# Transposing the feed-forward activations on VectorE in 32-partition blocks in place of TensorE

## The chip, the core and the metric

The kernel runs on one core of one Trainium2 chip. Its engines are TensorE (PE: matmuls; PEld is its weight load), VectorE (DVE), ScalarE (ACT), GpSimd (POOL) and SyncE (SP, which issues most DMAs). The metric is the time of one execution on the device, in microseconds; lower is better.

## The reference

One layer of a diffusion transformer over 256 latent tokens and 256 context tokens, width 2048, all in float32. The change touches only the feed-forward part, whose inner width is 5632:

```
def swiglu_sublayer(x, shift, scale, gate, norm_g, w_ff_gate, w_ff_up, w_ff_down):
    h = modulate(rms_norm(x, norm_g), shift, scale)
    return x + gate * ((jax.nn.silu(h @ w_ff_gate) * (h @ w_ff_up)) @ w_ff_down)
```

Before it stand the modulation vectors, one input projection, two kinds of attention, and the projections that merge them. `x` here has 256 rows, so `h @ w_ff_gate` is 256x2048 by 2048x5632.

## The kernel before

Every large product is done by `project`, in float32 split into two parts that TensorE takes at its quick float32 rate: a high part (a rounded copy) and the remainder. A product is the sum of three matmuls: high x high, high x remainder, remainder x high (`mm3`, lines 211 to 214, the names L212, L213 and L214 of the profile). L213 reads the weights' remainder.

Weights come in **weight tiles** of 256 rows by 512 columns (`load_w`, line 198). For each, SyncE issues a DMA into `wraw` (seven buffers), ScalarE makes the high part `whi` (L207, three buffers) and VectorE the remainder `wlo` (L208, three buffers). With each weight tile TensorE does twelve matmuls of 128x512: six for the first 128 tokens (tk 0), six for the others (tk 1). With three buffers, ScalarE can cast a tile only when TensorE has finished the tile three places ahead of it; VectorE follows ScalarE.

The feed-forward loop goes over eleven **groups** (`cg`) of 512 inner columns. A group has eight gate tiles and then eight up tiles. At the end of the gate tiles ScalarE writes silu of each token half to `act` (L941); at the end of the up tiles VectorE multiplies that by the up product (`u_evac`, L944). `act[tk]` is then 128 tokens by 512 inner columns. The down projection (four column groups of 22 weight tiles each) needs it with the inner columns on the partitions, so it has to be transposed, and then be split into the two parts again (`split`: ScalarE L217, VectorE L218) into `fT`. `turn` does this: four TensorE transposes of 128x128 against an identity matrix (L951) into PSUM, and the split out of PSUM. `after(n, fn)` and `tick` put it off by two weight tiles for tk 0 and three for tk 1, so that it stands in the next group's gate tiles (or in the down projection's first tiles, behind the last group).

From the third group on (`cg > 1`), VectorE also accumulates the modulation vector `a5` from a stream of weights, two pieces behind the gate tiles and two behind the up tiles (L393 for the first of a half, L395 for the others; written `ada` in the profile).

A scheduler places instructions on each engine's queue; each queue is run in order. In the tables that follow, the weight tiles of a group are counted from 0: tiles 0 to 7 are its gate tiles, 8 to 15 its up tiles.

Of the kernel before, what the change touches and what calls it, by code (L numbers as in the profile page):

```python
# [17 lines left out]
P = 128  # L18
D = 2048
NKT = D // P  # L20
# [14 lines left out]
CG = 512  # L35
# [5 lines left out]
TURN = 3  # L41
TURN2 = 5
# [3 lines left out]
def hybrid_block(ctx: ExitStack, tc: tile.TileContext, t: dict, out: bass.AP):  # L46
    nc = tc.nc
# [9 lines left out]
    def big_tile(name, dt=F32):  # L57
        return big.tile([P, 2048], dt, tag="big", name=name)

    def mm_ps(name="mm"):  # L60
        return psum.tile([P, CG], F32, tag="mm", bufs=4, name=name)

    def tp_ps(name="tp"):
        return psum.tile([P, CG], F32, tag="tp", bufs=2, name=name)
# [4 lines left out]
    def scratch(name, n=CG, dt=F32, tag="scr", bufs=3):  # L69
        return scr.tile([P, n], dt, tag=tag, bufs=bufs, name=name)  # L70
# [5 lines left out]
    ident = tab.tile([P, P], F32, name="ident")  # L76
# [121 lines left out]
    def load_w(src, r0, c0, nk=WK, in_big=False):  # L198
        raw = wp.tile([P, WK, CG], F32, tag="wraw", bufs=WRAW, name="wraw")
        nc.sync.dma_start(out=raw[:, 0:nk], in_=src[r0:r0 + nk * P, c0:c0 + CG].rearrange("(k p) c -> p k c", p=P))  # L200
        if in_big:
            both = big_tile("wbig", F32R).rearrange("p (h k c) -> p h k c", h=2, c=CG)
            hi, lo = both[:, 0], both[:, 1]
        else:
            hi = wp.tile([P, WK, CG], F32R, tag="whi", bufs=WHI, name="whi")
            lo = wp.tile([P, WK, CG], F32R, tag="wlo", bufs=WLO, name="wlo")
        last_hi.append(nc.scalar.copy(out=hi[:, 0:nk], in_=raw[:, 0:nk]))  # L207
        last_lo.append(nc.vector.tensor_tensor(out=lo[:, 0:nk], in0=raw[:, 0:nk], in1=hi[:, 0:nk].bitcast(F32), op=ALU.subtract))  # L208
        return hi, lo

    def mm3(ps, ah, al, wh, wl, first, last):
        nc.tensor.matmul(ps, lhsT=ah, rhs=wh, start=first, stop=False)  # L212
        nc.tensor.matmul(ps, lhsT=ah, rhs=wl, start=False, stop=False)  # L213
        return nc.tensor.matmul(ps, lhsT=al, rhs=wh, start=False, stop=last)  # L214

    def split(hi, lo, src):
        nc.scalar.copy(out=hi, in_=src)  # L217
        nc.vector.tensor_tensor(out=lo, in0=src, in1=hi.bitcast(F32), op=ALU.subtract)  # L218
# [165 lines left out]
    def ada_pieces(a, chunk):  # L384

        for kt, hf in [(kt, hf) for kt in range(NKT) for hf in range(2)]:
            wt = wp.tile([P, 1024], F32, tag="wraw", bufs=WRAW, name="wada2")
            nc.sync.dma_start(out=wt, in_=w_ada[kt * P:(kt + 1) * P, chunk * D + hf * 1024: chunk * D + (hf + 1) * 1024])
            dst = a[:, hf * 1024:(hf + 1) * 1024]
            yield None  # L390
            with tc.issue_after(last_lo[-1].ins):
                if kt == 0:
                    nc.vector.tensor_scalar(out=dst, in0=wt, scalar1=sc[:, 0, 0:1], scalar2=None, op0=ALU.mult)  # L393
                else:
                    nc.vector.scalar_tensor_tensor(out=dst, in0=wt, scalar=sc[:, 0, kt:kt + 1], in1=dst, op0=ALU.mult, op1=ALU.add)  # L395
# [94 lines left out]
    def take(gen, n):  # L490
        for _ in range(n):
            if next(gen, gen) is gen:
                return

    def drain(gen):
        for _ in gen:
            pass
# [9 lines left out]
    def after(n, fn):  # L507
        late.append([n, fn])

    def tick():  # L510
        for e in list(late):
            e[0] -= 1
            if e[0] <= 0:
                late.remove(e)
                e[1]()
# [59 lines left out]
    def project(src, hl, nkt, c0, evac, kt0=0, side=None, head=1, tail=1, hook=None):  # L575


        ps = [mm_ps() for _ in range(2)]
        nt = nkt // WK
        order = [(i, tk) for i in range(nt) for tk in range(2)]  # L580
        order[:2 * head] = [(i, tk) for tk in range(2) for i in range(head)]
        order[-2 * tail:] = [(i, tk) for tk in range(2) for i in range(nt - tail, nt)]
        wt = {}
        for n, (i, tk) in enumerate(order):
            if i not in wt:
                wt[i] = load_w(src, i * WK * P, c0, in_big=WHI <= i < head or nt - tail <= i < nt - WHI)
            wh, wl = wt[i]
            for j in range(WK):
                k = i * WK + j
                ah, al = hl.at(kt0 + k, tk * P, P)  # L590
                mm3(ps[tk], ah, al, wh[:, j], wl[:, j], k == 0, k == nkt - 1)
            if i == nt - 1 and (tail > 1 or tk == 1):
                for x in ([tk] if tail > 1 else range(2)):
                    evac(x, ps[x])
            if hook:
                hook(i, tk)
            if n % 2:
                tick()
                if side:
                    side()  # L600
                yield None
# [24 lines left out]
    def q_evac(qT, br):  # L626
        def f(tk, ps):
            o = norm_rope(ps, br, "q", tk)

            def turn():  # L630
                tp = tp_ps("qtp")
                for h in range(4):
                    nc.tensor.transpose(out=tp[:, h * P:(h + 1) * P], in_=o[:, h * P:(h + 1) * P], identity=ident)
                src = tp.rearrange("p (h q) -> p h q", h=4)
                split(qT[:, 0, :, tk * P:(tk + 1) * P], qT[:, 1, :, tk * P:(tk + 1) * P], src)
            after(5 + tk, turn)
        return f
# [79 lines left out]
    def unit(br, u):  # L717
        return (u // 4, u % 4) if br == "a" else (u // 8, u // 2 % 4)
# [59 lines left out]
    for n, (br, u) in enumerate(units):  # L778
        q = (br, unit(br, u)[0])
# [33 lines left out]
    for cg in range(4):  # L813
# [19 lines left out]
        def gated(tk, ps):  # L833
            g = gs[tk]
            nc.vector.tensor_tensor(out=g, in0=ps, in1=g, op=ALU.mult)
            nc.vector.tensor_tensor(out=m[tk], in0=m[tk], in1=g, op=ALU.add)
            after(2 + tk, turn(tk))

        def turn(tk, cg=cg, m=m):
            def f():  # L840
                tp = tp_ps("mtp")
                for j in range(4):
                    nc.tensor.transpose(out=tp[:, j * P:(j + 1) * P], in_=m[tk][:, j * P:(j + 1) * P], identity=ident)
                hi, lo = mT.four(cg, tk * P, P)
                split(hi, lo, tp.rearrange("p (h q) -> p h q", h=4))
            return f
# [34 lines left out]
    hT = Parts("hT", NKT)  # L881
# [49 lines left out]
    w_g, w_u, w_d = t["w_ff_gate"][0], t["w_ff_up"][0], t["w_ff_down"][0]  # L931
    NFT = DFF // P
    fT = Parts("fT", NFT)
    for cg in range(DFF // CG):
        if cg == 2:
            a5 = big_tile("ada5")
            a5_gen = ada_pieces(a5, 5)
        act = [scratch(f"act{tk}") for tk in range(2)]

        def g_evac(tk, ps):  # L940
            nc.scalar.activation(out=act[tk], in_=ps, func=AF.Silu)  # L941

        def u_evac(tk, ps):
            nc.vector.tensor_tensor(out=act[tk], in0=ps, in1=act[tk], op=ALU.mult)  # L944
            after(2 + tk, turn(tk))

        def turn(tk, cg=cg, act=act):
            def f():
                tp = tp_ps("ftp")
                for j in range(4):  # L950
                    nc.tensor.transpose(out=tp[:, j * P:(j + 1) * P], in_=act[tk][:, j * P:(j + 1) * P], identity=ident)  # L951
                hi, lo = fT.four(cg, tk * P, P)
                split(hi, lo, tp.rearrange("p (h q) -> p h q", h=4))
            return f

        drain(project(w_g, hT, NKT, cg * CG, g_evac, **(dict(head=TURN2, hook=head_hook) if cg == 0 else {})))
        if cg > 1:
            take(a5_gen, 2)
        drain(project(w_u, hT, NKT, cg * CG, u_evac))
        if cg > 1:  # L960
            take(a5_gen, 2)
    drain(a5_gen)
# [2 lines left out]
    for cg in range(4):  # L965
        def d_evac(tk, ps):
            xr = scratch("xr2", tag="p", bufs=4)
            nc.gpsimd.dma_start(out=xr, in_=x2_d[tk, :, cg * CG:(cg + 1) * CG])
            y = scratch("y")
            nc.vector.tensor_tensor(out=y, in0=ps, in1=a5[:, cg * CG:(cg + 1) * CG], op=ALU.mult)  # L970
            nc.vector.tensor_tensor(out=y, in0=y, in1=xr, op=ALU.add)
            (nc.sync if cg == 3 else nc.gpsimd).dma_start(out=out[0, tk * P:(tk + 1) * P, cg * CG:(cg + 1) * CG], in_=y)
        drain(project(w_d, fT, NFT, cg * CG, d_evac, tail=TURN if cg == 3 else 1))


_INS = ["x", "c", "ctx", "c_ctx", "w_ada", "b_ada", "norm1_g", "w_in", "q_norm_a", "k_norm_a", "q_norm_b", "k_norm_b",
# [32 lines left out]
```

## Time and profile before

| | |
|---|---|
| median of 3 runs | 1733.82 us (1732.61 to 1733.86) |
| span of the profiled execution, first to last instruction | 1730.7 us |
| TensorE busy | 1706.1 us (99% of the span) |
| VectorE busy | 1132.6 us (65%) |
| ScalarE busy | 775.0 us (45%) |
| granted TensorE clock, mean over the span | 0.998 |
| the four transposes of one tile (L951), as one run of work | 0.60 us, 22 times |

The time of the profiled execution as a run is not listed by itself; its span is 3.1 us below the median, and that is taken as the same for both kernels. A busy TensorE is not one at its peak, since matmuls overlap: a 128x512 matmul lasts 0.39 us in the trace and the next one starts about 0.227 us after it.

### The profile page before, as it was taken

The numbers are of one execution on the slowest core, as the hardware profiler recorded it, in microseconds if no ns is written. First come the engines' busy times: TensorE is split into PE (matmuls) and PEld (weight loads), VectorE is DVE, ScalarE is ACT, GpSimd is POOL, SyncE is SP. The second block draws the span as 40 slices with busy tenths as digits, with TensorE's granted clock in tenths as the row PEclk, the third lists the DMA queues.
The fourth block names the chain that finished last, engine by engine and source line by source line (L and its number), as shares of the span: only waits on it lengthen the run. The fifth ranks groups of instructions, "written<-read, shape, count | busy, mean of one in ns | idle before, by whom it ended". The sixth has DMA issues, their size and how long they took to land.

```text
span 1730.7 us, 21827 instructions
## 1 busy us (share of the span) xinstructions
PE 1706.1 (99%) x8150; PEld 1378.5 (80%) x8150; DVE 1132.6 (65%) x1428; ACT 775.0 (45%) x1063; POOL 135.5 (8%) x204
## 2 busy tenths in 40 slices
PE   7999999999999999999999999999999999999998
PEld 5667778887787788888888788888888888888887
DVE  5754668888788879796665754555565665454554
ACT  5222223245656556667544444444444444333332
POOL 2100001001131120002110100000000000000000
PEclk9999999999999999999999999999999999999999
DMA  9877785687766676777796766677777777666662
GB/s 263 300 242 265 233 319 174 201 271 235 252 189 202 212 265 217 247 227 248 249 323 222 237 180 190 201 237 241 234 242 234 240 236 231 208 213 197 221 205 88
DMA packets 192010, 397.69 MB, mean 230 GB/s; under 512 B 13504, under 2 KB 25872, under 8 KB 191392
## 3 DMA queue, kind: packets, MB, share of 16 engines
q1 hardware_dynamic: 183952, 369.71, 66.2%
q0 software_dynamic: 7952, 26.58, 4.8%
q8 instruction: 64, 1.05, 0.2%
q14 instruction: 42, 0.34, 0.1%
HBM read 385.72 MB, written 10.52 MB: 229 GB/s over the span
## 4 chain that ended last, share of the span: by engine, by line
PE 88%; DVE 5%; issue 3%; DMA 1%; ACT 1%; POOL 1%; SPq 0%; DVEq 0%; ACTq 0%; POOLq 0%
PE mm L212 26%; PE mm L213 26%; PE mm L214 26%; PE ada L268 2%; DVE wlo L208 1%; PE ptp L687 1%; PE o L705 1%; DMA wraw<-in_w_in_dram 1%; PE ftp L951 1%; PE s L667 1%; ACT whi L207 1%; PE o L213 0%; PE o L214 0%; PE o L212 0%; PE s L212 0%
## 5 line engine op out<-in xcount | busy, mean ns | idle before, releaser
L208 DVE TENSOR_TENSOR wlo<-wraw,whi 128x1024 fp32r<-128x1024 f32 (+1 forms) x506 | 611.6, 1210 | 460.2 <-ACT whi L207 458.8
L207 ACT CAST whi<-wraw 128x1024 fp32r<-128x1024 f32 (+1 forms) x506 | 527.7, 1043 | 796.6 <-PE mm L214 682.0
L213 PE MATMUL mm<-wlo,hT 128*128 128x512 f32 x696 | 271.0, 389 | 2.0 <-DVE wlo L208 2.0
L212 PE MATMUL mm<-whi,hT 128*128 128x512 f32 x696 | 272.8, 392 | 0.0
L214 PE MATMUL mm<-whi,hT 128*128 128x512 f32 x696 | 271.3, 390 | 0.1
L212 PE MATMUL mm<-whi,xT 128*128 128x512 f32 x640 | 257.2, 404 | 0.6 <-ACT whi L207 0.6
L213 PE MATMUL mm<-wlo,xT 128*128 128x512 f32 x640 | 251.5, 393 | 0.9 <-DVE wlo L208 0.9
L214 PE MATMUL mm<-whi,xT 128*128 128x512 f32 x640 | 250.5, 392 | 0.0
L213 PEld LDWEIGHTS mm<-wlo,hT 128*128 128x128 f32 x696 | 130.7, 188 | 28.8 <-DVE wlo L208 2.4
L214 PEld LDWEIGHTS mm<-whi,hT 128*128 128x128 f32 x696 | 130.6, 188 | 27.9 <-DVE hT L218 0.5
L395 DVE SCALAR_TENSOR_TENSOR ada<-wada,sc,ada 128x1024 f32<-128x1024 f32 x120 | 152.0, 1277 | 0.0
L212 PEld LDWEIGHTS mm<-whi,hT 128*128 128x128 f32 x696 | 130.7, 188 | 26.3
L212 PEld LDWEIGHTS mm<-whi,xT 128*128 128x128 f32 x640 | 120.1, 188 | 37.3 <-issue 9.8
L213 PEld LDWEIGHTS mm<-wlo,xT 128*128 128x128 f32 x640 | 120.8, 189 | 25.1 <-DVE wlo L208 2.4
L214 PEld LDWEIGHTS mm<-whi,xT 128*128 128x128 f32 x640 | 120.3, 188 | 25.4
L212 PE MATMUL mm<-whi,fT 128*128 128x512 f32 x352 | 137.2, 390 | 0.0
L214 PE MATMUL mm<-whi,fT 128*128 128x512 f32 x352 | 137.0, 389 | 0.0
L213 PE MATMUL mm<-wlo,fT 128*128 128x512 f32 x352 | 136.9, 389 | 0.0
L212 PEld LDWEIGHTS mm<-whi,fT 128*128 128x128 f32 x352 | 66.1, 188 | 14.5 <-issue 0.8
L212 PE MATMUL mm<-whi,cT 128*128 128x512 f32 x192 | 75.5, 393 | 1.8 <-ACT cT L344 1.8
L214 PEld LDWEIGHTS mm<-whi,fT 128*128 128x128 f32 x352 | 66.1, 188 | 13.9
L213 PEld LDWEIGHTS mm<-wlo,fT 128*128 128x128 f32 x352 | 66.1, 188 | 13.4
(237 smaller groups left out, 2115.2 us busy)
## 6 DMA issues: line engine op xcount, KB each, us to landing
wada<-in_w_ada_dram SPq DMA_DIRECT2D x192, 512.0 KB, 4.6
wraw<-in_w_in_dram SPq DMA_DIRECT2D x154, 512.0 KB, 4.6
wraw<-in_w_ff_gate_dram SPq DMA_DIRECT2D x88, 512.0 KB, 4.5
wraw<-in_w_ff_up_dram SPq DMA_DIRECT2D x88, 512.0 KB, 3.8
wraw<-in_w_ff_down_dram SPq DMA_DIRECT2D x88, 512.0 KB, 4.8
wraw<-in_w_br_a_dram SPq DMA_DIRECT2D x32, 512.0 KB, 5.0
wraw<-in_w_out_dram SPq DMA_DIRECT2D x32, 512.0 KB, 5.1
wraw<-in_w_br_b_dram SPq DMA_DIRECT2D x16, 512.0 KB, 5.4
```

Source lines behind the costliest of these rows:

```text
L207: last_hi.append(nc.scalar.copy(out=hi[:, 0:nk], in_=raw[:, 0:nk]))
L208: last_lo.append(nc.vector.tensor_tensor(out=lo[:, 0:nk], in0=raw[:, 0:nk], in1=hi[:, 0:nk].bitcast(F32), op=ALU.subtract))
L212: nc.tensor.matmul(ps, lhsT=ah, rhs=wh, start=first, stop=False)
L213: nc.tensor.matmul(ps, lhsT=ah, rhs=wl, start=False, stop=False)
L214: return nc.tensor.matmul(ps, lhsT=al, rhs=wh, start=False, stop=last)
L268: last_pe[0] = nc.tensor.matmul(aps[32 * g:32 * g + 32, 0:ncol], lhsT=cst[:, k, :], rhs=rhs, start=(k < 4), stop=(k >= NKT - 4))
L395: nc.vector.scalar_tensor_tensor(out=dst, in0=wt, scalar=sc[:, 0, kt:kt + 1], in1=dst, op0=ALU.mult, op1=ALU.add)
L667: nc.tensor.matmul(sps[i], lhsT=qT[rows, x, hh, tk * P:(tk + 1) * P], rhs=kT["b", grp][y][rows, hh, :], start=(n == 0), stop=(n == 2))
L687: nc.tensor.transpose(out=tp[:, kt * P:(kt + 1) * P], in_=p[:, kt * P:(kt + 1) * P], identity=ident)
L705: nc.tensor.matmul(op[:, 0:BV], lhsT=pT[:, kt, :], rhs=vb[:, kt, hh * BV:(hh + 1) * BV], start=(kt == 0), stop=(kt == 3))
L951: nc.tensor.transpose(out=tp[:, j * P:(j + 1) * P], in_=act[tk][:, j * P:(j + 1) * P], identity=ident)
```

## The change

`turn` goes. In its place each `act[tk]` gets a generator, `turned`, that issues sixteen VectorE transposes of 32 partitions by 4 x 32 elements. Instruction (a, b) reads partitions 32a to 32a+31, takes column block b out of each of the four 128-column chunks, turns each 32x32 block, and writes to partitions 32b to 32b+31 of an SBUF tile `fturn`. Then the split reads `fturn` in place of PSUM. `project` calls `blocks_turned` behind each weight tile (its `side` argument), which takes four steps of the oldest generator.

```
+    chain = []
+
+    def blocks_turned():
+
+        for _ in range(4):
+            if chain and next(chain[0], chain) is chain:
+                chain.pop(0)
+
+    def turned(src, dst_hi, dst_lo):
+
+        whole = scratch("fturn", tag="sq", bufs=2)
+        sv = src.rearrange("p (k b j) -> p b k j", k=4, b=4)
+        dv = whole.rearrange("p (k a j) -> p a k j", k=4, a=4)
+        for a in range(4):
+            for b in range(4):
+                nc.vector.transpose(out=dv[32 * b:32 * b + 32, a], in_=sv[32 * a:32 * a + 32, b])
+                yield None
+        split(dst_hi, dst_lo, whole.rearrange("p (k q) -> p k q", k=4))
+
...
         def u_evac(tk, ps):
             nc.vector.tensor_tensor(out=act[tk], in0=ps, in1=act[tk], op=ALU.mult)
-            after(2 + tk, turn(tk))
-
-        def turn(tk, cg=cg, act=act):
-            def f():
-                tp = tp_ps("ftp")
-                for j in range(4):
-                    nc.tensor.transpose(out=tp[:, j * P:(j + 1) * P], in_=act[tk][:, j * P:(j + 1) * P], identity=ident)
-                hi, lo = fT.four(cg, tk * P, P)
-                split(hi, lo, tp.rearrange("p (h q) -> p h q", h=4))
-            return f
-
-        drain(project(w_g, hT, NKT, cg * CG, g_evac, **(dict(head=TURN2, hook=head_hook) if cg == 0 else {})))
+            chain.append(turned(act[tk], *fT.four(cg, tk * P, P)))
+
+        drain(project(w_g, hT, NKT, cg * CG, g_evac, side=blocks_turned, **(dict(head=TURN2, hook=head_hook) if cg == 0 else {})))
...
-        drain(project(w_u, hT, NKT, cg * CG, u_evac))
+        drain(project(w_u, hT, NKT, cg * CG, u_evac, side=blocks_turned))
...
-        drain(project(w_d, fT, NFT, cg * CG, d_evac, tail=TURN if cg == 3 else 1))
+        drain(project(w_d, fT, NFT, cg * CG, d_evac, side=blocks_turned, tail=TURN if cg == 3 else 1))
```

The new lines have the numbers L949 (transpose) and L963 (the multiplication that was L944). On TensorE the 22 runs of four L951 are gone and nothing else moves. What VectorE and ScalarE get to do, and in which order, is the scheduler's.

**VectorE, from the end of the third group's up tiles into the fourth group's gate tiles, before.** The first L208 rows are for tiles 2 and 3 of the fourth group.

```order
L944 TENSOR_TENSOR act_9592<-mm,act_9592 128x512
L944 TENSOR_TENSOR act_9593<-mm,act_9593 128x512
L208 TENSOR_TENSOR wlo<-wraw,whi 128x1024 x2
L218 TENSOR_TENSOR fT_9943<-ftp,fT_9943 128x4x128
L208 TENSOR_TENSOR wlo<-wraw,whi 128x1024
L218 TENSOR_TENSOR fT_9943<-ftp,fT_9943 128x4x128
L208 TENSOR_TENSOR wlo<-wraw,whi 128x1024 x3
L395 SCALAR_TENSOR_TENSOR ada_9591<-wada_9914,sc,ada_9591 128x1024
L395 SCALAR_TENSOR_TENSOR ada_9591<-wada_10082,sc,ada_9591 128x1024
L208 TENSOR_TENSOR wlo<-wraw,whi 128x1024 x8
```

Between two remainders there is at most one L218, or the two L395.

**The same place on VectorE with the change**, behind the two multiplications (`act_9622` is tk 0, `act_9623` is tk 1).

```order
L949 STREAM_TRANSPOSE fturn<-act_9622 32x4x32 x12
L208 TENSOR_TENSOR wlo<-wraw,whi 128x1024
L949 STREAM_TRANSPOSE fturn<-act_9622 32x4x32 x4
L208 TENSOR_TENSOR wlo<-wraw,whi 128x1024
L218 TENSOR_TENSOR fT_9957<-fturn,fT_9957 128x4x128
L949 STREAM_TRANSPOSE fturn<-act_9623 32x4x32 x3
L208 TENSOR_TENSOR wlo<-wraw,whi 128x1024
L949 STREAM_TRANSPOSE fturn<-act_9623 32x4x32 x4
L208 TENSOR_TENSOR wlo<-wraw,whi 128x1024
L949 STREAM_TRANSPOSE fturn<-act_9623 32x4x32 x8
L208 TENSOR_TENSOR wlo<-wraw,whi 128x1024
L949 STREAM_TRANSPOSE fturn<-act_9623 32x4x32
```

The five L208 rows are for tiles 2 to 6. The code asks for four transposes behind each weight tile; the scheduler puts twelve in one run ahead of tile 2's remainder, and eight ahead of tile 6's.

**What follows directly on VectorE with the change:**

```order
L218 TENSOR_TENSOR fT_9957<-fturn,fT_9957 128x4x128
L208 TENSOR_TENSOR wlo<-wraw,whi 128x1024
L395 SCALAR_TENSOR_TENSOR ada_9621<-wada_9968,sc,ada_9621 128x1024
L395 SCALAR_TENSOR_TENSOR ada_9621<-wada_10154,sc,ada_9621 128x1024
L208 TENSOR_TENSOR wlo<-wraw,whi 128x1024 x8
```

The second split has moved from ahead of tile 5's remainder to ahead of tile 7's, and the two L395, which stand where they stood, now come directly behind it. No wait stands between the transposes of one run.

**ScalarE, from one group's silu to the next one's, before:**

```order
L941 ACTIVATE act_9592<-mm 128x512
L941 ACTIVATE act_9593<-mm 128x512
L207 CAST whi<-wraw 128x1024 x10
L217 CAST fT_9943<-ftp 128x4x128
L207 CAST whi<-wraw 128x1024
L217 CAST fT_9943<-ftp 128x4x128
L207 CAST whi<-wraw 128x1024 x5
```

**and with the change:**

```order
L960 ACTIVATE act_9622<-mm 128x512
L960 ACTIVATE act_9623<-mm 128x512
L207 CAST whi<-wraw 128x1024 x10
L217 CAST fT_9957<-fturn 128x4x128
L207 CAST whi<-wraw 128x1024 x3
L217 CAST fT_9957<-fturn 128x4x128
L207 CAST whi<-wraw 128x1024 x3
```

The tenth L207 is tile 3 of the next group. The second L217 has moved from behind tile 4's cast to behind tile 6's; both L217 now wait for VectorE's sixteenth transpose, and the casts of tiles 4 and 7 stand behind them.

## The prediction

> **What bounds the kernel now.** I read first how busy each engine is, then the same for the middle of the feed-forward loop alone (stretches of the span; columns are length, busy time of each engine with its instructions, granted clock, DMA share), and then the order of time.
>
> ```profile
> PE 1706.1 (99%) x8150; PEld 1378.5 (80%) x8150; DVE 1132.6 (65%) x1428; ACT 775.0 (45%) x1063; POOL 135.5 (8%) x204
> ...
> core 0: us, PE busy (x) PEld busy (x) DVE busy (x) ACT busy (x) POOL busy (x), PEclk, DMA share, GB/s
> ...
> 1172.00:1477.00 305.00, 305.00 (x1374) 252.56 (x1374) 179.59 (x164) 130.33 (x138) 2.04 (x4) 1.00 0.75 236
> ```
>
> In those 305 us TensorE never stops, at full clock, while VectorE works 59% of the time. So an instruction taken from TensorE shortens the kernel by its whole place in the queue, as long as nobody makes TensorE wait in its stead. The order of time, around the first group's transposes (start, duration, engine, line, idle time ahead of it):
>
> ```profile
> 1037.69 1.23 DVE L208 TENSOR_TENSOR wlo<-wraw,whi 128x1024 fp32r<-128x1024 f32 x1 [1.50 <-ACT whi L207]
> ...
> 1038.83 1.28 DVE L944 TENSOR_TENSOR act<-mm,act 128x512 f32<-128x512 f32 x2
> ...
> 1039.12 0.39 PE L212 MATMUL mm<-whi,hT 128*128 128x512 f32 x1
> ...
> 1039.32 1.05 ACT L207 CAST whi<-wraw 128x1024 fp32r<-128x1024 f32 x1 [1.67 <-PE mm L214]
> ...
> 1040.41 1.23 DVE L208 TENSOR_TENSOR wlo<-wraw,whi 128x1024 fp32r<-128x1024 f32 x1 [0.29 <-ACT whi L207]
> ...
> 1041.39 0.39 PE L213 MATMUL mm<-wlo,hT 128*128 128x512 f32 x1
> ...
> 1041.62 0.39 PE L214 MATMUL mm<-whi,hT 128*128 128x512 f32 x1
> ...
> 1041.85 0.60 PE L951 MATMUL ftp<-ident,act 128*128 128x128 f32 x4
> 1042.04 1.05 ACT L207 CAST whi<-wraw 128x1024 fp32r<-128x1024 f32 x1 [1.67 <-PE mm L214]
> ...
> 1042.20 0.47 PE L212 MATMUL mm<-whi,hT 128*128 128x512 f32 x1
> ...
> 1042.51 0.39 PE L213 MATMUL mm<-wlo,hT 128*128 128x512 f32 x1
> ```
>
> Tile 0 of the second group starts at 1039.12 and has twelve matmuls, so without transposes tile 1 would start 12 x 0.227 = 2.72 us later. At 1039.32 ScalarE casts tile 2, when tile 7 of the up product is out of its buffer; VectorE follows at 1040.41 and ends at 1041.64, while tile 2 starts at 1039.12 + 5.44 = 1044.56. So VectorE can be some 3 us late with a remainder; that is the whole cover.
>
> **What goes: the transposes on TensorE.** From the L214 at 1041.62 to the second matmul behind the transposes, at 1042.51, are 0.89 us; two matmul places would be 0.45. A run of four costs 0.44 us of TensorE's queue, 0.88 a group, and the 22 runs 9.7 us. The split stays; it now reads SBUF:
>
> ```profile
> L217 ACT CAST fT<-ftp x22: 579/580/581, 1043.0 to 1492.0; 128x512 fp32r<-128x512 f32 x22
> L218 DVE TENSOR_TENSOR fT<-ftp,fT x22: 681/683/685, 1044.3 to 1493.3; 128x512 fp32r<-128x512 f32 x22
> ...
> L217 ACT CAST cT<-hx 128x512 fp32r<-128x512 f32 x7 | 4.3, 623 | 0.1
> ```
>
> ScalarE's half becomes 0.62 us (the row whose source is in SBUF, in place of 0.58), VectorE's stays at 0.69.
>
> **What comes: 352 transposes on VectorE.** The trace has none. Rows with 128 elements a partition, and rows on how instructions follow each other:
>
> ```profile
> L108 DVE TENSOR_TENSOR ce<-ce,cin 32x128 f32<-32x128 f32 x1 | 0.3, 280 | 0.0
> ...
> L710 DVE SCALAR_TENSOR_TENSOR on<-o,rstdo,gsub 128x128 f32<-128x128 f32 x16 | 5.6, 350 | 7.4 <-POOL rstdo L128 7.3
> ...
> L343 DVE TENSOR_SCALAR hx<-xtp,mod,mod 128x128 f32<-128x128 f32 x4 | 1.6, 408 | 1.9 <-PE xtp L339 1.9
> ...
> 15.78 0.16 DVE L142 TENSOR_REDUCE ss_row<-ss_part 128x1 f32<-128x4 f32 x1
> 15.97 0.15 DVE L127 TENSOR_SCALAR rstd_row<-ss_row 128x1 f32<-128x1 f32 x1
> ...
> 18.83 0.29 DVE L345 TENSOR_TENSOR xT<-hx,xT 128x128 fp32r<-128x128 f32 x1
> 19.04 1.27 DVE L148 TENSOR_SCALAR tok<-tok,rstd_row 128x512 f32<-128x512 f32 x3
> ```
>
> Let T be the time from one transpose to the next. The lower bound is 0.21 us: a 128-element instruction at 18.83 is followed 0.21 us later by one that doesn't need it, with 0.08 of overlap. If nothing overlaps, T is the 0.28 of the one row of 32x128 plus the 0.03 from an end (15.94) to the next start (15.97): 0.31. The upper bound is 0.41 (the 128x128 row out of PSUM), with 0.35 between. I take 0.31. The shape is that of the 280 ns row, and every overlap in the trace is between instructions that begin on partition 0 and go element by element; here each one writes to another 32 partitions than the last, and the first column of a block can only leave when its last row is in.
>
> The Trainium skill's "VectorE: DVE Perf Modes", section "Two Vector instructions with no wait between them", says that an instruction is held until all earlier ones have finished when it starts on other partitions than the last in the same memory; all sixteen write elsewhere than their predecessor. The trace's nearest pair (0.21, overlapped) begins on the same partitions and can't test it; by the rule the lower bound falls away, by the pair the whole 9.7 us is won. The same page's section "The three transpose paths" gives 311 ns for 128x128 in bf16, the only price of a transpose there is; with that as T the sum would be the one below.
>
> **The walk through VectorE's queue.** Time zero is the start of tile 0 of a group (1039.12); tile k starts at 2.72k plus what was lost. Two things set the loss: how late a remainder ends, and when TensorE goes on after one. For the second the trace has a row:
>
> ```profile
> 993.73 1.21 DVE L208 TENSOR_TENSOR wlo<-wraw,whi 128x1024 fp32r<-128x1024 f32 x1
> ...
> 994.99 0.50 PE L213 MATMUL mm<-wlo,hT 128*128 128x512 f32 x1 [2.00 <-DVE wlo L208]
> ...
> 995.33 0.39 PE L214 MATMUL mm<-whi,hT 128*128 128x512 f32 x1
> ```
>
> The remainder ends at 994.94; the next but one matmul starts 0.39 later. In an undisturbed tile that one starts 0.45 behind the tile's start. So TensorE loses what the remainder ends later than 0.06 behind the tile's start. For VectorE's instructions I take duration less 0.09 to the next start (1037.69 to 1038.83 for 1.23), and 0.04 from an end to an instruction that waited for it. In the order of the queue, with T = 0.31:
>
> - The multiplications end at 0.99 (1038.83 plus 1.28 is 1040.11). Twelve transposes, started at 0.91, end at 4.63. Tile 2's remainder ends at 5.86; tile 2 starts at 5.44: 0.36 lost.
> - Four transposes end at 7.0, tile 3's remainder at 8.25; tile 3 starts at 8.52: in time. ScalarE's split of tk 0 runs from 7.06 to 7.68, VectorE's ends at 8.86.
> - Three transposes, tile 4's remainder ends at 10.94 (start 11.24); four, tile 5's ends at 13.33 (start 13.96): in time.
> - Eight transposes end at 15.7, tile 6's remainder at 16.96; tile 6 starts at 16.68: 0.22 lost.
> - The last transpose ends at 17.2. ScalarE's second split waits for it (17.23 to 17.85), and behind it stands the cast of tile 7, to 18.82; the remainder ends at 20.09, tile 7 starts at 19.62: 0.41 lost. Here a wait on ScalarE, not VectorE's work alone, sets the end.
> - In groups with `a5`, two pieces come next and end at 22.5; tile 8's remainder ends at 23.64, tile 8 starts at 22.75: 0.83 lost. Their price:
>
> ```profile
> 1122.97 1.28 DVE L395 SCALAR_TENSOR_TENSOR ada<-wada,sc,ada 128x1024 f32<-128x1024 f32 x1
> 1124.17 1.22 DVE L208 TENSOR_TENSOR wlo<-wraw,whi 128x1024 fp32r<-128x1024 f32 x1
> ```
>
> From tile 9 on VectorE has caught up (24.79 against 26.30). A crossing with two pieces loses 1.82 us and saves 0.88; one without loses 0.99. Of the eleven crossings seven have two pieces; two have none (into group 1 and into the down projection), and two have one short or single piece, which the slack takes. Sum: 7 x (1.82 - 0.88) + 4 x (0.99 - 0.88) = +7.0 us on the span of 1730.7, so 1737.7, and with the 3.1 us between span and median **1740.8 us**.
>
> Costed at nothing: the loads of `wraw` (SyncE waits for VectorE's remainder before it refills one of seven buffers; a load lands in 4.8 us in the slowest of these stages, by the median, and seven tiles are 19 us, so a delay of 4 is covered), `act` and `fturn` (their next use is most of a group later), and the last group's transposes (done by tile 8 of 22; the down projection needs that group at tile 20). POOL's queue isn't touched.
>
> ```profile
> wraw<-in_w_ff_down_dram SPq DMA_DIRECT2D x88, 512.0 KB, 4.8
> ```
>
> **Rivals.** The same walk with other values of T gives them all; losses per crossing with and without pieces are, at 0.25: 0 and 0; 0.28: 0.88 and 0.05; 0.30: 1.50 and 0.67; 0.35: 3.10 and 2.27; 0.41: 5.02 and 4.19.
>
> - *Overlapped transposes.* With T up to 0.25 no remainder is late, and the whole 9.7 us are won: 1724.1. For it: the pair at 18.83, and VectorE's 41% of idle time. Against it: what I said on blocks and partitions. It decides below T = 0.29, where gain and loss are equal; at 0.28 the sum is 4 x (0.05 - 0.88) = -3.3, 1730.5.
> - *A dearer transpose.* At 0.35 the sum is 7 x 2.22 + 4 x 1.39 = +21, 1755; at 0.41 it is 7 x 4.14 + 4 x 3.31 = +42, 1776. For it: rows L710 and L343. Against: both have operands in PSUM, and the transpose has none.
> - *The clock.* Waits could cost TensorE its clock on top. After the wait of 2.0 us that ended at 994.99 the clock was halved for 2.5 us; after one of 1.29 us it wasn't (the last row has TensorE's busy time, the clock 1.00 and DMA alone).
>
> ```profile
> 996.30:998.80 2.50, 2.50 (x7) 1.87 (x6) 2.19 (x4) 0.00 (x0) 0.27 (x1) 0.50 0.80 269
> ...
> 741.96 0.50 PE L214 MATMUL mm<-whi,oT 128*128 128x512 f32 x1 [1.29 <-DVE oT L218]
> ...
> 742.00:744.00 2.00, 2.00 (x9) 1.00 0.00 0
> ```
>
> My longest wait is 0.83, so I don't count on it; 1.25 us at each of eleven crossings would make 1740.8 + 14 = 1755.
>
> **How the numbers follow.** T between 0.30 and 0.33 (+3 to +14): 0.38, the likeliest, with 1740.8. T up to 0.25: 0.27. Between 0.25 and 0.30: 0.17, half of it faster by more than 0.2% (3.5 us, about what a measurement of this kernel can tell from no change). Dearer: 0.12. Clock: 0.06. Faster: 0.27 + 0.08 = 0.35. Same: the other 0.09 and 0.04 from the low end of the first case: 0.13. Slower: 0.52. The range goes from 1723, just below the whole gain, to 1756, which takes in T = 0.35 and the clock; left out are the dearest transposes and what I overlooked, about 0.13. My forecast's own case is 1737 to 1748.
>
> **What would show it.** L951 gone and TensorE's matmul count down by 88; transposes of 0.28 to 0.31 with starts 0.31 apart; TensorE waiting for `wlo` in tiles 2, 6, 7 and 8 of each group, with some 1.8 us a crossing, and waits of ScalarE's L217 on the transposes. No waits at all and starts 0.2 apart would show the first rival; waits in every tile from 2 to 8 the second. The prediction is wrong if T is off by 0.02 us: each 0.01 moves the time by about 3.5 us.

## The result and the profile after

| | before | after |
|---|---|---|
| median of 5 runs each | 1733.82 us (1732.61 to 1734.24) | 1747.77 us (1745.33 to 1749.64) |
| span of the profiled execution | 1730.7 us | 1746.0 us |
| granted TensorE clock, mean | 0.998 | 0.998 |

The changed kernel is slower: 1.0081 times the time before, with a 95% interval of 1.0069 to 1.0093, or +13.95 us by the medians. The forecast was +7.0.

Of the 15.3 us between the two spans, 2.3 lie ahead of the change: tile 0 of the second group starts at 1039.12 before and at 1041.41 after. From there to the start of the last matmul are 685.90 us before (to 1725.02) and 698.94 after (to 1740.35). So 13.0 us is what the traces have to explain. This stretch, from tile 0 of the second group to the last matmul, is given for the kernels below too. What lies ahead of it is the same program but scatters: in nine of the ten traces tile 0 starts between 1038.63 and 1041.41, and in the second experiment, which clears two buffers first, at 1043.46. The prediction's 3.1 us between span and median hold some of that scatter as well; the changed kernel's span is 1.8 us below the time of its own run.

First how busy each engine is (busy us, share, instructions), then the same stretch as before in the stretches of the span:

```profile
PE 1707.2 (98%) x8062; PEld 1365.2 (78%) x8062; DVE 1236.0 (71%) x1780; ACT 774.5 (44%) x1063; POOL 134.8 (8%) x204
...
1172.00:1477.00 305.00, 296.82 (x1275) 236.72 (x1274) 242.91 (x386) 125.44 (x133) 2.03 (x4) 1.00 0.69 226
```

TensorE has 88 matmuls fewer, but in the 305 us in which it never stopped before, it now stands idle for 8.2, at full clock. The waits from the feed-forward loop on (instruction, what it waited for, us in total, times, longest) name the reason:

```profile
ACT fT L217 <- DVE fturn L949: 92.6, 22, 5.3
...
PEld mm L213 <- DVE wlo L208: 27.7, 38, 1.1
...
PE mm L213 <- DVE wlo L208: 11.7, 38, 0.7
```

TensorE waits 38 times for a remainder. One crossing, from the third into the fourth group, in order of time on VectorE, with ScalarE's second split and the cast behind it. Tile 0 starts at 1131.76.

```profile
1131.47 1.28 DVE L963 TENSOR_TENSOR act<-mm,act 128x512 f32<-128x512 f32 x2
1132.67 3.77 DVE L949 STREAM_TRANSPOSE fturn<-act 32x128 f32<-32x128 f32 x12
1136.47 1.23 DVE L208 TENSOR_TENSOR wlo<-wraw,whi 128x1024 fp32r<-128x1024 f32 x1
1137.72 1.26 DVE L949 STREAM_TRANSPOSE fturn<-act 32x128 f32<-32x128 f32 x4
1139.02 1.22 DVE L208 TENSOR_TENSOR wlo<-wraw,whi 128x1024 fp32r<-128x1024 f32 x1
1140.16 0.69 DVE L218 TENSOR_TENSOR fT<-fturn,fT 128x512 fp32r<-128x512 f32 x1
1140.76 0.92 DVE L949 STREAM_TRANSPOSE fturn<-act 32x128 f32<-32x128 f32 x3
1141.72 1.23 DVE L208 TENSOR_TENSOR wlo<-wraw,whi 128x1024 fp32r<-128x1024 f32 x1
1142.97 1.25 DVE L949 STREAM_TRANSPOSE fturn<-act 32x128 f32<-32x128 f32 x4
1144.26 1.23 DVE L208 TENSOR_TENSOR wlo<-wraw,whi 128x1024 fp32r<-128x1024 f32 x1
1145.52 2.52 DVE L949 STREAM_TRANSPOSE fturn<-act 32x128 f32<-32x128 f32 x8
1148.07 1.23 DVE L208 TENSOR_TENSOR wlo<-wraw,whi 128x1024 fp32r<-128x1024 f32 x1
1149.33 0.31 DVE L949 STREAM_TRANSPOSE fturn<-act 32x128 f32<-32x128 f32 x1
...
1149.67 0.62 ACT L217 CAST fT<-fturn 128x512 fp32r<-128x512 f32 x1 [5.32 <-DVE fturn L949]
1150.20 3.10 ACT L207 CAST whi<-wraw 128x1024 fp32r<-128x1024 f32 x3
...
1150.32 0.69 DVE L218 TENSOR_TENSOR fT<-fturn,fT 128x512 fp32r<-128x512 f32 x1 [0.69 <-ACT fT L217]
1151.28 1.22 DVE L208 TENSOR_TENSOR wlo<-wraw,whi 128x1024 fp32r<-128x1024 f32 x1 [0.26 <-ACT whi L207]
1152.42 2.47 DVE L395 SCALAR_TENSOR_TENSOR ada<-wada,sc,ada 128x1024 f32<-128x1024 f32 x2
```

Twelve transposes in 3.77 us: they follow one another 0.315 us apart, with no overlap. The L208 rows are for tiles 2 to 7. The same crossing on TensorE:

```profile
1137.20 0.39 PE L212 MATMUL mm<-whi,hT 128*128 128x512 f32 x1
1137.75 0.50 PE L213 MATMUL mm<-wlo,hT 128*128 128x512 f32 x1 [0.16 <-DVE wlo L208]
1138.08 0.39 PE L214 MATMUL mm<-whi,hT 128*128 128x512 f32 x1
...
1149.35 0.50 PE L213 MATMUL mm<-wlo,hT 128*128 128x512 f32 x1 [0.43 <-DVE wlo L208]
...
1152.55 0.50 PE L213 MATMUL mm<-wlo,hT 128*128 128x512 f32 x1 [0.17 <-DVE wlo L208]
...
1156.08 0.50 PE L213 MATMUL mm<-wlo,hT 128*128 128x512 f32 x1 [0.51 <-DVE wlo L208]
```

These are tiles 2, 6, 7 and 8. In tile 2 the third matmul starts 0.88 us behind the first, where two places are 0.45: 0.43 lost, of which the row shows 0.16 as idle. So each wait costs its idle time plus 0.27, since the matmuls ahead of the wait and behind it no longer overlap; in tiles 6, 7 and 8 the difference is the same within 0.02. For the 38 waits that is 11.7 + 38 x 0.27 = 22.0 us lost, against the 9.7 saved: +12.3 of the 13.0.

The 38 are tiles 2, 6 and 7 in the ten crossings between two groups, tile 8 in the seven with two pieces, and in the crossing into the down projection tile 6 alone:

```profile
1517.59 0.50 PE L213 MATMUL mm<-wlo,fT 128*128 128x512 f32 x1 [0.69 <-DVE wlo L208]
```

### The profile page after: what moved, and what is told of

The parts are those of the page before. It is cut to its first block, busy times and chain, and to the rows that moved or that the text cites. A ratio compares the mean times of both kernels' runs of the same rounds, so it can differ in the third digit from the quotient of the medians.

```text
span 1746.0 us, 22002 instructions
## 1 busy us (share of the span) xinstructions
PE 1707.2 (98%) x8062; PEld 1365.2 (78%) x8062; DVE 1236.0 (71%) x1780; ACT 774.5 (44%) x1063; POOL 134.8 (8%) x204
## 4 chain that ended last, share of the span: by engine, by line
PE 72%; DVE 16%; issue 5%; DMA 3%; ACT 2%; POOL 1%; SPq 0%; ACTq 0%; DVEq 0%; POOLq 0%
PE mm L213 22%; PE mm L214 21%; PE mm L212 21%; DVE wlo L208 6%; DVE fturn L949 5%; DMA wraw<-in_w_in_dram 3%; ACT whi L207 2%; PE ada L268 1%; PE ptp L687 1%; PE o L705 1%; DVE act L963 1%; PE s L667 1%; PE o L213 0%; PE o L214 0%; PE o L212 0%
## 5 line engine op out<-in xcount | busy, mean ns | idle before, releaser
L208 DVE TENSOR_TENSOR wlo<-wraw,whi 128x1024 fp32r<-128x1024 f32 (+1 forms) x506 | 609.8, 1210 | 360.1 <-ACT whi L207 356.8
L207 ACT CAST whi<-wraw 128x1024 fp32r<-128x1024 f32 (+1 forms) x506 | 526.3, 1043 | 715.0 <-PE mm L214 592.2
L213 PE MATMUL mm<-wlo,hT 128*128 128x512 f32 x696 | 275.6, 396 | 13.0 <-DVE wlo L208 13.0
L395 DVE SCALAR_TENSOR_TENSOR ada<-wada,sc,ada 128x1024 f32<-128x1024 f32 x120 | 152.0, 1277 | 0.0
L949 DVE STREAM_TRANSPOSE fturn<-act 32x128 f32<-32x128 f32 x352 | 106.4, 302 | 5.3
L212 PEld LDWEIGHTS mm<-whi,fT 128*128 128x128 f32 x352 | 66.1, 188 | 14.7 <-issue 0.8
```

The lines of the kernel that those rows point to most:

```text
L949: nc.vector.transpose(out=dv[32 * b:32 * b + 32, a], in_=sv[32 * a:32 * a + 32, b])
```

## The experiments

The theory was that of the prediction: TensorE's saving is real, and the bunched, unoverlapped transposes make remainders late for more than that. The rivals: VectorE's added work itself is too much; the saving is less than it seems; the a5 pieces or ScalarE's queue have no part in it; writing to other partitions is not what keeps the transposes apart. In the diffs `-` and `+` are against the changed kernel. The median of the kernel before was 1734.2 us beside the first four kernels below and 1734.6 beside the others.

**No transposes on any engine.**

```
-            chain.append(turned(act[tk], *fT.four(cg, tk * P, P)))
+            hi, lo = fT.four(cg, tk * P, P)
+            after(2 + tk, lambda tk=tk, act=act, hi=hi, lo=lo: split(hi, lo, act[tk].rearrange("p (h q) -> p h q", h=4)))
```

> No engine transposes the activations: the split reads act as it stands, on the old schedule (this leaves the transposition out). Both theories: the 22 runs of four TensorE transposes were worth 22 x 0.44 = 9.7 us, so about 1724.1, and TensorE waits for no weight remainder in the feed-forward loop. If the gain was mis-sized (if TensorE had given part of it back elsewhere in any case), it is above 1728.

Measured: 1723.41 us (1722.82 to 1727.02), 0.9943 times before (0.9929 to 0.9956). TensorE doesn't wait for a remainder anywhere in the loop. The gain of taking the transposes off TensorE is real and of the size that the prediction had: 9.9 us by the ratio (7.6 to 12.3), 9.7 forecast. The stretch takes 675.56 us, 10.3 less than before, so a run of four was worth 0.47 us and not 0.44.

**All sixteen transposes on the same partitions.**

```
-        whole = scratch("fturn", tag="sq", bufs=2)
+        whole = wholes[0]
+        wholes.reverse()
...
-                nc.vector.transpose(out=dv[32 * b:32 * b + 32, a], in_=sv[32 * a:32 * a + 32, b])
+                nc.vector.transpose(out=dv[0:32, a], in_=sv[0:32, b])
```

(`wholes` are two `fturn` buffers, cleared once on GpSimd and used in turn.)

> All sixteen transposes read and write partitions 0 to 31 (this leaves three quarters of each turned tile out, they stay zero); number, size and type of the instructions are the change's. Theory: transposes start one behind the other without overlap because each goes to other partitions than the last. Then they now overlap, start some 0.22 us apart for the same 0.30 us, no remainder is late, and the time is about 1724. Rival: a transpose never overlaps with the next one, whatever its partitions. Then they stay 0.315 apart and the time stays at about 1748.

Measured: 1723.35 us (1720.7 to 1726.42), 0.9933 (0.9919 to 0.9947): as fast as without any transposes, and the stretch takes the same 675.56 us. The instructions of `fturn` as a group (count, shortest/median/longest ns), and the order of time on VectorE:

```profile
L953 DVE STREAM_TRANSPOSE fturn<-act x352: 256/257/300, 1044.4 to 1492.0; 32x128 f32<-32x128 f32 x176
...
1131.41 1.83 DVE L953 STREAM_TRANSPOSE fturn<-act 32x128 f32<-32x128 f32 x9
1133.17 1.17 DVE L208 TENSOR_TENSOR wlo<-wraw,whi 128x1024 fp32r<-128x1024 f32 x1
1134.28 1.25 DVE L953 STREAM_TRANSPOSE fturn<-act 32x128 f32<-32x128 f32 x6
1135.47 1.17 DVE L208 TENSOR_TENSOR wlo<-wraw,whi 128x1024 fp32r<-128x1024 f32 x1
```

Nine transposes of 0.257 take 1.83 us, so starts are (1.83 - 0.257) / 8 = 0.197 apart on the mean instead of 0.315. The remainder starts 0.07 before the last transpose ends (1131.41 + 1.83 against 1133.17), and the next transpose 0.06 before the remainder ends; in the changed kernel both start 0.02 to 0.03 after. The scheduler also put nine instead of twelve transposes ahead of tile 2's remainder here. That alone couldn't free tile 6: ahead of its remainder stand 31 transposes in both kernels. Since everything here begins on partition 0, the run doesn't tell whether transposes that stay on other partitions overlap too.

**Pieces of a5 three weight tiles later**, behind the third up tile instead of directly behind the gate tiles.

```
-        if cg > 1:
-            take(a5_gen, 2)
-        drain(project(w_u, hT, NKT, cg * CG, u_evac, side=blocks_turned))
+        for i, _ in enumerate(project(w_u, hT, NKT, cg * CG, u_evac, side=blocks_turned)):
+            if cg > 1 and i == 2:
+                take(a5_gen, 2)
```

> The two a5 pieces behind the gate tiles move to behind the third up tile; all else is the change's. Theory (late remainders, place by place): only tile 8's wait goes, 0.8 us at each of the seven crossings with two pieces, 5.6 us in all, to about 1742; waits in tiles 2, 6 and 7 stay as they are. Rival (VectorE has too much to do between two groups, wherever it stands): the pieces are still to be done there, and the time stays within 2 us of 1748.

Measured: 1740.84 us (1738.47 to 1742.06), 1.0034 (1.0021 to 1.0046). The waits:

```profile
PEld mm L213 <- DVE wlo L208: 21.2, 31, 1.1
...
PE mm L213 <- DVE wlo L208: 8.2, 31, 0.7
```

31 waits instead of 38: just the seven of tile 8 are gone, and with them 6.9 us by the medians and 5.7 in the stretch, which takes 693.25 us (seven waits of 0.78, as shown above, are 5.5). So tile 8's wait is the pieces'; the other three stand without them.

**Transposes spread and put off.** The chain starts three weight tiles later (`after(4, ...)` counts the tile in which it is called; the expectation says two), so that a group's first four transposes stand behind tile 2's remainder. Every transpose is held behind the latest remainder, which keeps runs at four.

```
-                nc.vector.transpose(out=dv[32 * b:32 * b + 32, a], in_=sv[32 * a:32 * a + 32, b])
+                with tc.issue_after(last_lo[-1].ins):
+                    nc.vector.transpose(out=dv[32 * b:32 * b + 32, a], in_=sv[32 * a:32 * a + 32, b])
...
-            chain.append(turned(act[tk], *fT.four(cg, tk * P, P)))
+            gen = turned(act[tk], *fT.four(cg, tk * P, P))
+            after(4, lambda gen=gen: chain.append(gen))
```

> The same sixteen transposes a tile, but started two weight tiles later and pinned, four each behind the remainder of the weight tile last issued, so that no run is longer than four or five. Theory (bunching): 1.26 us of transposes and 1.23 us of a remainder fit into a weight tile's 2.72 us, no remainder is late, and the whole 9.7 us is won: about 1724. Rival (VectorE's added 110 us, or its use of the memory, slow TensorE however they are spread): 1740 or more.

Measured: 1722.85 us (1720.66 to 1726.35), 0.9934 (0.992 to 0.9948). This version beats both kernels, and it is as fast as the one without transposes; the stretch takes 675.56 us once more. How busy the engines are, and VectorE at the same crossing:

```profile
PE 1695.5 (99%) x8062; PEld 1369.7 (80%) x8062; DVE 1238.2 (72%) x1780; ACT 776.2 (45%) x1063; POOL 135.3 (8%) x204
...
1128.22 1.22 DVE L208 TENSOR_TENSOR wlo<-wraw,whi 128x1024 fp32r<-128x1024 f32 x1 [0.30 <-ACT whi L207]
1129.36 1.24 DVE L950 STREAM_TRANSPOSE fturn<-act 32x128 f32<-32x128 f32 x4
1130.94 1.23 DVE L208 TENSOR_TENSOR wlo<-wraw,whi 128x1024 fp32r<-128x1024 f32 x1 [0.34 <-ACT whi L207]
1132.20 1.25 DVE L950 STREAM_TRANSPOSE fturn<-act 32x128 f32<-32x128 f32 x4
```

VectorE works as long as in the changed kernel (1238.2 us against 1236.0) with the same 352 transposes 0.315 apart. But remainder and four transposes now take 2.4 us of each tile's 2.72, VectorE waits 0.3 for the next cast, and TensorE waits for no remainder. So it isn't the amount of work on VectorE that made the change slow, but where it stands.

**Only the hold behind the latest remainder**, without the later start (the first of the two edits above).

> The change with the transposes only pinned behind the remainder of the weight tile last issued; the start isn't put off, so the run of twelve ahead of tile 2 stays (tiles 0 and 1 have their remainders by then) and the rest is spread by fours. Theory (walk through VectorE's queue with 0.315 us from start to start and no overlap where a remainder and a transpose follow each other): tile 2 loses 0.4 us at every crossing, tiles 6 and 7 nothing, tile 8 some 1.2 us at the crossings with two a5 pieces: 3.7 us above the kernel before, about 1737.5. Rival (pinning alone cures it, the later start isn't needed): 1724.

Measured: 1734.47 us (1733.15 to 1736.3), 1.0004 (0.9995 to 1.0012). Weight loads that waited at the crossing from the third group:

```profile
1133.64 0.19 PEld L213 LDWEIGHTS mm<-wlo,hT 128*128 128x128 f32 x1 [0.58 <-DVE wlo L208]
...
1151.10 0.19 PEld L213 LDWEIGHTS mm<-wlo,hT 128*128 128x128 f32 x1 [1.27 <-DVE wlo L208]
```

The run of eight ahead of tile 6 is gone, and tiles 6 and 7 no longer wait. Twelve still stand ahead of tile 2's remainder, and the pieces and a split ahead of tile 8's. The hold takes most of the loss back: the stretch takes 688.12 us, 2.2 more than before. The later start on top of it brings the rest of the gain; what it would do without the hold, no run shows.

**The split later.** Both halves of a split come three weight tiles later than in the change, held behind the latest cast and the latest remainder.

```
-        split(dst_hi, dst_lo, whole.rearrange("p (k q) -> p k q", k=4))
+        def parts():
+            src = whole.rearrange("p (k q) -> p k q", k=4)
+            with tc.issue_after(last_hi[-1].ins):
+                nc.scalar.copy(out=dst_hi, in_=src)
+            with tc.issue_after(last_lo[-1].ins):
+                nc.vector.tensor_tensor(out=dst_lo, in0=src, in1=dst_hi.bitcast(F32), op=ALU.subtract)
+        after(3, parts)
```

> The transposes stand as in the change, in the same runs, but both halves of the split come three weight tiles later, pinned behind the newest cast and remainder, so that ScalarE's cast of a weight tile never stands behind a wait for transposes. Theory: the waits at tiles 7 and 8 (0.5 and 0.8 us) hang on ScalarE's queue and go, tile 6 keeps a half (0.44), tile 2 its 0.4: 1.2 us above the kernel before, about 1735. Rival (VectorE's transposes alone make the remainders late, ScalarE only follows): 1744 or more.

Measured: 1733.62 us (1730.29 to 1739.67), 0.9992 (0.9981 to 1.0002).

```profile
1133.60 0.19 PEld L213 LDWEIGHTS mm<-wlo,hT 128*128 128x128 f32 x1 [0.57 <-DVE wlo L208]
...
1144.92 0.19 PEld L213 LDWEIGHTS mm<-wlo,hT 128*128 128x128 f32 x1 [0.53 <-DVE wlo L208]
```

The stretch takes 685.06 us, 0.8 less than before. The expectation took the transposes to stay in the change's runs. They don't: between the remainders of tiles 4 and 6 they now stand in runs of seven and six,

```profile
1138.23 2.20 DVE L949 STREAM_TRANSPOSE fturn<-act 32x128 f32<-32x128 f32 x7
1140.45 1.23 DVE L208 TENSOR_TENSOR wlo<-wraw,whi 128x1024 fp32r<-128x1024 f32 x1
1141.71 1.90 DVE L949 STREAM_TRANSPOSE fturn<-act 32x128 f32<-32x128 f32 x6
1143.64 1.23 DVE L208 TENSOR_TENSOR wlo<-wraw,whi 128x1024 fp32r<-128x1024 f32 x1
```

so the last one ends ahead of tile 6's remainder and not behind it.

Tile 2 waits as before, tile 6 less, and tiles 7 and 8 not at all, although the pieces stand where they stood. With no cast queued behind a split that waits for transposes, VectorE gets through in time. The edit moves ScalarE's half, VectorE's half and, by the scheduler, the last transposes together, so their shares aren't told apart.

**Half on VectorE.** tk 0 by VectorE as in the change, tk 1 by TensorE as before (`turn` as in the kernel before).

```
-            chain.append(turned(act[tk], *fT.four(cg, tk * P, P)))
+            if tk == 0:
+                chain.append(turned(act[tk], *fT.four(cg, tk * P, P)))
+            else:
+                after(2 + tk, turn(tk))
```

> Only the first token half of each group (tk 0) is turned on VectorE, the second on TensorE as before. Theory: 11 x 0.44 = 4.8 us are saved; the run of twelve ahead of tile 2 is there and would lose 0.4 us, but TensorE's own transposes of the second half stand just ahead of tile 2 and give it 0.44 more time, so nothing is lost: about 1729. Rival (each turned tile costs its share of the 24 us that were lost in all): 1734 + 7 = 1741.

Measured: 1727.43 us (1726.92 to 1728.89), 0.9957 (0.9945 to 0.9969). The twelve transposes still stand ahead of tile 2's remainder; TensorE's work there:

```profile
1132.70 1.23 DVE L208 TENSOR_TENSOR wlo<-wraw,whi 128x1024 fp32r<-128x1024 f32 x1
...
1133.44 0.60 PE L973 MATMUL ftp<-ident,act 128*128 128x128 f32 x4
1133.79 0.48 PE L212 MATMUL mm<-whi,hT 128*128 128x512 f32 x1
1134.11 0.39 PE L213 MATMUL mm<-wlo,hT 128*128 128x512 f32 x1
```

TensorE's own transposes of tk 1 fall just ahead of tile 2 and give its remainder, which ends at 1133.93, the time that it lacked. No matmul waits. Half the saving, 4.9 us, was expected on that; the stretch, 680.67 us, is 5.2 shorter than before, and the medians say 5.4 to 9.5 by the interval.

**Written partition kept over four transposes, read partition changed each time.**

```
-        for a in range(4):
-            for b in range(4):
+        for b in range(4):
+            for a in range(4):
```

> The two loops over a and b are swapped: four transposes in turn write to the same 32 partitions and read from changing ones; the result is the same. Theory A (a change of the partitions read or of those written holds the next transpose): starts stay 0.315 us apart, time about 1748. Theory B (only a change of the partitions written holds it): three of four overlap, starts some 0.22 us apart on the mean, no remainder is late, about 1724.

Measured: 1745.95 us (1743.83 to 1747.15), 1.0062 (1.0048 to 1.0076).

```profile
L949 DVE STREAM_TRANSPOSE fturn<-act x352: 289/303/309, 1041.1 to 1514.7; 32x128 f32<-32x128 f32 x176
...
1131.50 3.77 DVE L949 STREAM_TRANSPOSE fturn<-act 32x128 f32<-32x128 f32 x12
```

Nothing changes (the stretch takes 698.87 us against 698.94): a change of the partitions that are read holds a transpose as a change of those written does.

## Why the prediction was right in direction and short by half

- **What bounds the kernel, and the gain.** Right: without transposes 9.9 us are won (9.7 forecast; 10.3 in the stretch), and the version with the transposes spread and put off wins the same.
- **The price of a transpose, T.** 0.31 was taken between 0.21 and 0.41; the trace has 0.303 long and 0.315 apart. By the prediction's own 3.5 us for each 0.01, that is worth 1.7 us. The first rival (overlapped transposes) is refuted for this kernel, and the pair of rows that spoke for it does hold where the partitions stay: 0.197 apart in the second experiment. The Trainium skill's "VectorE: DVE Perf Modes", section "Two Vector instructions with no wait between them", says that an instruction waits until all earlier ones have finished if the partitions where its input or its output begins are in another quarter than the last time; the second and the eighth experiment agree with it (0.197 with none changed, 0.315 with the input's changed each time). By that rule a transpose behind a remainder, and a remainder behind a transpose, are held as well. A tile's first transpose isn't, since it reads and writes from partition 0 as the instruction ahead of it does; so fifteen of the sixteen are held.
- **The dearer transpose and the clock.** Neither came: T is 0.315, tiles 3 to 5 wait in no crossing, and the clock is the same 0.998.
- **The walk through the queue.** The tiles are the forecast ones, 2, 6, 7 and 8. Their losses:

| tile | 2 | 6 | 7 | 8 | crossing with pieces | without |
|---|---|---|---|---|---|---|
| forecast, us | 0.36 | 0.22 | 0.41 | 0.83 | 1.82 | 0.99 |
| measured, us | 0.43 | 0.70 | 0.44 | 0.78 | 2.35 | 1.57 |

("Without" is tiles 2, 6 and 7 of this crossing.) The crossing into the down projection is unlike the others: its one wait costs 0.69 + 0.27 = 0.96. With the measured losses the prediction's own sum is 7 x (2.35 - 0.88) + 3 x (1.57 - 0.88) + (0.96 - 0.88) = +12.4 of the 13.0 between the traces.

The step that failed is the size of tile 6's loss, which alone makes 10 x 0.48 = 4.8 us of the 6.0 by which the sum was short. More than half of what made it too small is one term of the walk: "For VectorE's instructions I take duration less 0.09 to the next start". It was read from two elementwise instructions in a row and used at every change between remainder and transposes. In the trace after, the remainder that starts at 1136.47 ends at 1137.70 and the transposes follow at 1137.72: 0.11 later than the prediction had it. Where both begin on partition 0 the 0.09 stands: the L218 at 1140.16 ends at 1140.85, and the first transpose of the next tile starts at 1140.76. Up to tile 6's remainder there are three runs of transposes directly behind a remainder (3 x 0.11 = 0.33), 31 transposes of 0.315 instead of 0.31 (0.16), and five remainders that start some 0.03 later than the steps of T allow (0.13): 0.62 together. Tile 6's remainder ends 17.54 behind tile 0's start (1149.30 less 1131.76), where 16.96 was forecast: 0.58 in fact. Tile 2 is only 0.08 of that late and loses 0.07 more, which gives the later tiles that much; the rest falls on tile 6, where no slack is left, and makes 0.22 into 0.70. The prediction argued from the partitions for T, within a run, and not at its ends. The second experiment, where starts at these changes come 0.06 to 0.07 before the end again, shows that it is the partitions.

- **ScalarE's queue and the pieces.** Borne out: in the trace after, tile 7's remainder waits for a cast that stands behind the second split (1149.67 to 1151.28), with the split later the waits of tiles 7 and 8 go, and with the pieces later that of tile 8 alone. The share of ScalarE's queue by itself wasn't isolated.
- **Costed at nothing.** Loads, buffers and the down projection's need of the last group cost nothing that shows: TensorE has no such wait from the loop on.

What stays open is small. By the medians four kernels came out 1 to 3 us below their expectation; the stretch, without the scatter ahead of it, leaves two. Later pieces gain 5.7 there (5.6 expected) and half the work 5.2 (4.8). The hold alone comes out 2.2 above the kernel before, where 3.7 was expected: the saving is 10.3 and not 9.7, tile 2 loses nothing in the crossing into the down projection, and tile 8's wait costs 1.1 (0.80 to 0.85 idle, plus 0.27) and not 1.2. The later split comes out 0.8 below it, where 1.2 above was expected; its other runs of transposes weren't in the expectation, and how much they explain wasn't followed further.

## What to carry to other kernels

Work moved to an engine with idle time is free only if it fits, tile by tile, into the gap before the next thing the busy engine needs: here 352 instructions cost 23.4 us against no transposes at all (698.94 less 675.56) in runs of twelve and eight, and nothing in runs of at most four. Look at the order in which the scheduler really places them, and pin it when it bunches them. When a queue without slack is walked by hand, get the gap at each kind of change from rows of that kind, since 0.1 us at a change, met several times, all falls on the first tile that has no slack.

## What the runs showed of the hardware

Behind another transpose on the same partitions, a transpose is recorded as 257 ns and starts 0.197 us after the one before; where the partitions that it reads or writes change, it is recorded as 303 ns and starts 0.315 us after. So a block transpose over all partitions pays 0.12 us an instruction for changing partitions, in either loop order. The same shows at the ends of a run: next to a 128x1024 remainder, starts come 0.06 to 0.09 us before the other's end where both begin on partition 0, and 0.02 to 0.03 after it where they don't. All these overlaps are between instructions that begin on partition 0.
